# A hybrid attention block: products of coming units drawn in behind each transpose

## The chip, the cores and the metric

The kernel runs on one core of one Trainium2 chip. The metric is the device time of one execution in microseconds. The core has five engines with a queue each, which run side by side and wait for one another by semaphores: TensorE (PE; its weight loads are shown as PEld), VectorE (DVE), ScalarE (ACT), GpSimd (POOL) and SyncE (SP, which only issues DMA transfers here). An engine takes the instructions of its queue in the order in which the program has them.

## The reference, cut to what matters

One decoder layer on x of 512 rows by 1024 columns, in float32. A normalised copy h of x is multiplied by one wide matrix; its columns feed two attention branches (FoX, with forget terms, and MoBA, block-sparse), 8 heads of 64 columns each, a SiLU gate for each branch, and two merging gates.

```
h = rms_norm(x, norm_g)
fq, fk, fv, fz, mq, mk, mv, mz, ga, gb, fl = split_cols(h @ w_in, sizes)
y_fox  = from_heads(fox_attention(q, k, v, log_f)) * silu(fz)
...
y_moba = from_heads(moba_attention(q, k, v)) * silu(mz)
merged = sigmoid(ga + b_gate[0]) * (y_fox @ w_fox) + sigmoid(gb + b_gate[1]) * (y_moba @ w_moba)
out = x + merged @ w_out
```

## The kernel before

Matrices are kept as a high and a low part (tiles ending in h and l, or hi and lo), and a product in float32 is made of three matmuls: high by high, high by low, low by high.

The work comes in stages: the first loads and the normalisation; the first q, k, z and v columns (to about 60 us); attention; the gates with the second merge; the output projection.

**Attention.** Sixteen heads are done in four groups of four (FoX halves a and b, MoBA halves a and b), two pairs of heads in each. For a pair, `Tr` transposes its q and k columns (four 128x128 transposes into the PSUM tile `p_qT`, four into `p_kT`, L530 and L532) and ScalarE and VectorE make `QS`, `KH` and `KL` of them (L539 to L547; `Q` is cast at L557 for FoX). For a head, `Aa` makes four logits tiles `lg` of 128 rows by 128, 256, 384 and 512 columns (L572, L573), VectorE adds the mask and finds the row minimum (L575), ScalarE takes the exponential (L577). Then `Bb` transposes the ten non-zero 128x128 blocks of the probabilities (`blk`, L617): four into `p_a`, four into `p_b`, two into `p_cc`. ScalarE copies each of these tiles into a high part `pth` (L623), VectorE makes the low part `ptl` (L624), and eight matmuls with the values make `pv` (L627, L628), which is summed into `ypair` (L652, L653). So a head has 10 transposes and a pair 8: 16 x 10 + 8 x 8 = 224.

**PSUM.** The tiles lie in banks that are shared by tag: three banks for `tp` (`p_qT`, `p_kT`, `p_a`, `p_b`, `p_cc`, `p_ri`), two for `lg`, two for `pj` (the units below), one for `pv`. A tile can be written only when the engines have read the tile that was in its bank.

**Units.** Between the steps of attention stand units of other work: `unit` (128 rows of a 256-column projection, 24 matmuls, L315 to L317, tile `pj_...`), `unit_z` (half of a SiLU gate, 24 matmuls of 512 columns, L414 to L416, `pz_...`) and `unit_f` (128 columns of the first merge, 12 matmuls of 512 columns, L696 to L698, `pf...`). `filler` turns the units of a list of names into functions: each first calls `pump`, which issues weight loads on SP and the splitting of weights (ACT L141, DVE L143: `wh_...`, `wl_...`) up to three steps ahead, then makes all its matmuls and the evacuation of its tile. `inter` alternates a group's steps with its units. The plan is: group fa with fqb, fkb, fvb, mqa; fb with mka, mva, mza; ma with mqb, mkb, mvb; mb with mzb, wf0, wf1, wf2. After the last group `seq(["wf3"])` makes the last unit pair of the first merge.

**Order.** The program is written in the order of these calls, and a scheduler then orders each engine's instructions by its own estimate of time; `tc.issue_after(i)` keeps what is issued inside the block behind instruction `i` on its engine. So products of a unit and transposes already mix in the program before, but most transposes stand in runs of 2 to 10.

Of the kernel before, what the change touches and what calls it, by code (L numbers as in the profile page):

```python
# [13 lines left out]
P = 128  # L14
# [3 lines left out]
KT = D // P  # L18
# [11 lines left out]
def fox_moba_kernel(ctx: ExitStack, tc, xT, x, w_in, w_fl, w_fox, w_moba, w_out, cst, rope, out):  # L30
# [274 lines left out]
        for i, (a, b) in enumerate(pairs):  # L305
            T.matmul(o, a, b, start=(i == 0), stop=(i == n - 1))

    def unit_mm(p, name, t, hfs=(0, 1), first=True, last=True):
        n = 264 if name == "fka" else CW
        for hf in hfs:  # L310
            hi, lo = chunks[name][hf]
            for k in range(4):
                kk = 4 * hf + k
                st = slice(t * P, (t + 1) * P)
                T.matmul(p[:, :n], Gh[:, kk, st], hi[:, k, :n], start=(kk == 0), stop=False)  # L315
                T.matmul(p[:, :n], Gh[:, kk, st], lo[:, k, :n], start=False, stop=False)
                T.matmul(p[:, :n], Gl[:, kk, st], hi[:, k, :n], start=False, stop=(kk == KT - 1))  # L317

    def evac_qk(p, name, t):
        if name not in QN:  # L320
# [75 lines left out]
    def unit(name, t):  # L396
        def go():
            p = pj(f"pj_{name}{t}")
            unit_mm(p, name, t)
# [7 lines left out]
    def tr_mm(p, name, c):  # L407
        cc = slice(c * P, (c + 1) * P)
        for hf in range(2):
            hi, lo = chunks[name][hf]  # L410
            for k in range(4):
                kk = 4 * hf + k
                gh, gl = Z[kk] if name[0] == "f" else (Gh[:, kk, :], Gl[:, kk, :])
                T.matmul(p, hi[:, k, cc], gh, start=(kk == 0), stop=False)  # L414
                T.matmul(p, hi[:, k, cc], gl, start=False, stop=False)
                T.matmul(p, lo[:, k, cc], gh, start=False, stop=(kk == KT - 1))  # L416

    ZS = {}

# [2 lines left out]
    def unit_z(name, c):  # L422
        def go():
            p = (tp if name == "fzb" else pj)(f"pz_{name}{c}")
            tr_mm(p, name, c)
# [12 lines left out]

    LR = con.tile([64, S], F32R, name="LR")
# [77 lines left out]
    def attn_group(br, half, gq, gk):  # L517
# [8 lines left out]
        def Tr(pr):  # L526
            def go():
                pq, pk = tp("p_qT"), tp("p_kT")
                for t in range(NT):
                    T.transpose(pq[:, t * P:(t + 1) * P], qn[:, t, pr * P:(pr + 1) * P], ident)  # L530
                for t in range(NT):
                    T.transpose(pk[:, t * P:(t + 1) * P], kn[:, t, pr * P:(pr + 1) * P], ident)  # L532
                for o in range(2):
                    h = 2 * pr + o
                    me, ot = (slice(0, HD), slice(HD, P)) if o == 0 else (slice(HD, P), slice(0, HD))
                    qs = t2("qs", 4, "QS", dt=F32R)
                    kh = t2("qs", 4, "KH", dt=F32R)
                    kl = KLt[o][pr]
                    A.activation(qs[me, :], pq[me, :], AF.Copy, scale=gq[me, :])  # L539
                    V.scalar_tensor_tensor(qs[ot, :], pq[me, :], gq[me, :], qs[me, :].bitcast(F32),  # L540
                                           op0=OP.mult, op1=OP.subtract)
                    A.activation(kh[me, :], pk[me, :], AF.Copy, scale=gk[me, :])
                    if direct:
                        A.activation(kh[ot, :], pk[me, :], AF.Copy, scale=gk[me, :])  # L544
                    else:
                        nc.scalar.dma_start(out=kh[ot, :].bitcast(F32), in_=kh[me, :].bitcast(F32))
                    V.scalar_tensor_tensor(kl[me, :], pk[me, :], gk[me, :], kh[me, :].bitcast(F32),  # L547
                                           op0=OP.mult, op1=OP.subtract)
                    q2 = qs
                    if fox:  # L550
                        q2 = Q2t[o]
                        lr = slice(HD, HD + 4) if o == 0 else slice(0, 4)
                        hh = hb + h
                        nc.sync.dma_start(out=q2[lr, :].bitcast(F32), in_=LR[hh:32:8, :].bitcast(F32))
                        nc.sync.dma_start(out=kl[lr, :].bitcast(F32), in_=LR[32 + hh:64:8, :].bitcast(F32))
                        if direct:
                            V.tensor_copy(q2[me, :], qs[me, :].bitcast(F32))  # L557
# [52 lines left out]
        def Bb(h):  # L610
            def go():
# [2 lines left out]
                pv = pst("pv", 1, "pv")  # L614

                def blk(dst, i, j):
                    T.transpose(dst, pts[i][:, j * P:(j + 1) * P], ident)  # L617
# [70 lines left out]

    FS, MG = {}, {}

    def br_mm(p, name, br, c):
        hi, lo = chunks[name][0]
        cc = slice(c * P, (c + 1) * P)
        for k in range(4):
            yh, yl = Y[br, k]
            T.matmul(p, hi[:, k, cc], yh, start=(k == 0), stop=False)  # L696
            T.matmul(p, hi[:, k, cc], yl, start=False, stop=False)  # L697
            T.matmul(p, lo[:, k, cc], yh, start=False, stop=(k == 3))  # L698

    def unit_f(i, c):  # L700
        def go():
            j = 2 * i + c
            p = pj(f"pf{j}")
            br_mm(p, f"wf{i}", "f", c)
# [128 lines left out]
    def merge_a(i, c):  # L833
        if True:
            j = 2 * i + c
            p = pj(f"pm{j}")
            br_mm(p, f"wm{i}", "m", c)
# [183 lines left out]
            return [unit_z(name, c) for c in range(2)]  # L1021
        return [unit(name, t) for t in range(4)]

    def filler(names):
        res = []
        for nm in names:
            for n, u in enumerate(units(nm)):
                def go(i=first_prep[nm] + (n if nm[0] == "G" else 0), u=u):
                    pump(i)
                    u()  # L1030
                res.append(go)
        return res

    def inter(a, b):
# [30 lines left out]
    for k, u in enumerate(fz):  # L1065
        u()
        if k < 3:
# [169 lines left out]
```

## Time and profile before

| what | value |
|---|---|
| median of 3 runs | 425.61 us (425.08 to 425.87) |
| the profiled execution's own time | 425.94 us |
| its span, first to last instruction | 424.2 us |
| granted TensorE clock | 0.999 |
| instructions | 7682 |
| HBM read, written | 48.11 MB, 6.32 MB |

Lines of a timeline give the start and the duration of an instruction (or of a run of like ones, xN) in microseconds, its engine, its line in the kernel, the tile it writes and those that it reads, and its shape. The duration of a matmul reaches to where its result is written, so matmuls overlap one another: what one costs TensorE is read from start to start. A line of a group gives the count, the busy time in us, the mean of one in ns, and the idle time of its engine just before with what ended it.

### The profile page before, as it was taken

The page shows a single profiled execution, that of the slowest core. Times are in us where ns is not written, and L with a number is a line of the kernel's source. Part 1 is how long each engine was busy: PE and PEld are TensorE (multiplying, and loading weights), DVE is VectorE, ACT ScalarE, POOL GpSimd, SP SyncE. Part 2 cuts the span into 40 slices and gives each one's busy share as a digit, 9 for nine tenths or more (in the row PEclk, how much of TensorE's full clock was granted, in tenths as well). Part 3 has the DMA queues.
Part 4 walks back from the last instruction along what each step waited for, and adds up shares of the span by engine and source line. Part 5 has one row for each costly group of instructions (what it writes and reads, how often), then busy time and mean ns, then how long its engine had stood idle before and what let it go on. Part 6 is the DMA issues. An engine that isn't in the chain of part 4 may idle for free.

```text
span 424.2 us, 7682 instructions
## 1 busy us (share of the span) xinstructions
PE 417.8 (98%) x2913; PEld 388.6 (92%) x2913; DVE 327.4 (77%) x574; ACT 279.2 (66%) x527; POOL 103.8 (24%) x120
## 2 busy tenths in 40 slices
PE   8999999999999999999999999999999999999996
PEld 6998899999999998899998888899999989988885
DVE  3779977799967778678666679767979698689883
ACT  4976326778777878569757687656756535686450
POOL 1065630225235550015660100340000000022230
PEclk9999999999999999999999999999999999999999
DMA  7972334667253033212032310673052703697484
GB/s 233 392 281 87 112 100 111 181 206 199 74 176 114 26 102 100 80 45 99 27 100 68 106 53 27 229 250 117 24 178 62 236 2 110 208 259 118 99 140 159
DMA packets 24340, 56.10 MB, mean 132 GB/s; under 512 B 2808, under 2 KB 7600, under 8 KB 24304
## 3 DMA queue, kind: packets, MB, share of 16 engines
q1 hardware_dynamic: 13392, 38.11, 27.9%
q0 software_dynamic: 3392, 8.39, 8.7%
q10 hardware_dynamic: 7520, 9.11, 6.7%
q8 instruction: 23, 0.38, 0.4%
q14 instruction: 13, 0.11, 0.1%
HBM read 48.11 MB, written 6.32 MB: 128 GB/s over the span
## 4 chain that ended last, share of the span: by engine, by line
PE 96%; DMA 1%; SPq 0%; DVE 0%; issue 0%; ACT 0%
PE pb_GB L770 3%; PE pb_GA L770 3%; PE pb_GA L767 3%; PE pb_GB L767 3%; PE pb_GB L769 3%; PE pb_GA L769 3%; PE po L958 3%; PE po L957 3%; PE po L956 3%; PE pv L628 2%; PE lg L573 2%; PE pv L627 2%; PE lg L572 2%; PE pf L697 2%; PE pf L696 2%; PE pm L698 2%
## 5 line engine op out<-in xcount | busy, mean ns | idle before, releaser
L343 POOL TENSOR_TENSOR ff<-ss,mh 128x8 f32<-128x8 f32 x16 | 31.6, 1981 | 71.4 <-DVE ss L341 62.9
L575 DVE CUSTOM_DVE_ANT_0 p<-lg,mask 128x128 f32<-128x128 f32 (+1 forms) x64 | 30.9, 487 | 16.1 <-PE lg L573 15.6
L577 ACT ACTIVATE p<-p,negm 128x128 f32<-128x128 f32 (+1 forms) x64 | 35.7, 559 | 10.9 <-DVE negm L575 10.0
L905 POOL DMA_DIRECT2D wr_o<-in_w_out_dram x4 | 4.9, 1294 | 95.5 <-ACT wr_o L904 95.5
L143 DVE TENSOR_TENSOR wl_GA<-wr_ga,wh_GA 128x1024 fp32r<-128x1024 f32 x14 | 16.9, 1223 | 5.8 <-ACT wh_GA L141 3.9
L141 ACT ACTIVATE wh_GA<-wr_ga 128x1024 fp32r<-128x1024 f32 x14 | 14.7, 1061 | 9.9 <-PE pb_GA L769 5.1
L141 ACT ACTIVATE wh_GB<-wr_gb 128x1024 fp32r<-128x1024 f32 x14 | 14.6, 1059 | 9.5 <-PE pm L697 3.5
L918 ACT ACTIVATE wh_o<-wr_o 128x1024 fp32r<-128x1024 f32 x14 | 14.8, 1060 | 7.9 <-PE pb_GB L769 2.8
L572 PE MATMUL lg<-KH,QS 128*128 128x128 f32 (+1 forms) x64 | 20.0, 324 | 0.0
L919 DVE TENSOR_TENSOR wl_o<-wr_o,wh_o 128x1024 fp32r<-128x1024 f32 x14 | 17.0, 1222 | 3.8 <-ACT wh_o L918 3.8
L143 DVE TENSOR_TENSOR wl_GB<-wr_gb,wh_GB 128x1024 fp32r<-128x1024 f32 x14 | 16.9, 1222 | 3.5 <-ACT wh_GB L141 3.5
L653 DVE TENSOR_TENSOR ypair<-pv,ysh 64x512 f32<-64x512 f32 x16 | 11.0, 687 | 6.7 <-ACT ysh L652 6.3
L547 DVE SCALAR_TENSOR_TENSOR KL<-p_kT,cs,KH 64x512 fp32r<-64x512 f32 x16 | 12.0, 749 | 3.4 <-ACT KH L544 3.2
L652 ACT ACTIVATE ysh<-pv 64x512 f32<-64x512 f32 x16 | 9.5, 594 | 7.3 <-PE pv L628 4.2
L624 DVE TENSOR_TENSOR ptl<-p_a,pth 128x512 fp32r<-128x512 f32 x16 | 11.0, 685 | 4.2 <-ACT pth L623 4.2
L337 DVE TENSOR_REDUCE ss<-sq 128x8 f32<-128x512 f32 x16 | 10.9, 681 | 4.0 <-ACT sq L336 3.9
L767 PE MATMUL pb_GA<-Gh,wh_GA 128*128 128x256 f32 x48 | 13.6, 284 | 0.0
L769 PE MATMUL pb_GA<-Gl,wh_GA 128*128 128x256 f32 x48 | 13.5, 281 | 0.0
L770 PE MATMUL pb_GA<-Gh,wl_GA 128*128 128x256 f32 x48 | 13.5, 281 | 0.0
L770 PE MATMUL pb_GB<-Gh,wl_GB 128*128 128x256 f32 x48 | 13.5, 281 | 0.0
L769 PE MATMUL pb_GB<-Gl,wh_GB 128*128 128x256 f32 x48 | 13.4, 281 | 0.0
L767 PE MATMUL pb_GB<-Gh,wh_GB 128*128 128x256 f32 x48 | 13.3, 281 | 0.0
(461 smaller groups left out, 1801.8 us busy)
## 6 DMA issues: line engine op xcount, KB each, us to landing
wr_ga<-in_w_in_dram SPq DMA_DIRECT2D x8, 512.0 KB, 3.8
wr_gb<-in_w_in_dram SPq DMA_DIRECT2D x8, 512.0 KB, 4.6
wr_o<-in_w_out_dram SPq DMA_DIRECT2D x8, 512.0 KB, 11.4
xt<-in_xT_dram SPq DMA_DIRECT2D x8, 256.0 KB, 7.3
x<-in_x_dram SPq DMA_DIRECT2D x8, 256.0 KB, 6.0
s_dramh<-sum_sh ACTq DMA_DIRECT2D x8, 256.0 KB, 5.6
s_draml<-sum_sl ACTq DMA_DIRECT2D x8, 256.0 KB, 2.5
wr_wf<-in_w_fox_dram SPq DMA_DIRECT2D x4, 512.0 KB, 3.2
```

The source lines that it names most:

```text
L141: A.activation(hi[:, :, 0:n], src, AF.Copy)
L143: eng.tensor_tensor(out=lo[:, q, 0:n], in0=src[:, q], in1=hi[:, q, 0:n].bitcast(F32), op=OP.subtract)
L343: G.tensor_tensor(out=f2, in0=ss.rearrange("p t h -> p (t h)"), in1=mh, op=OP.pow)
L572: T.matmul(lg[:, :n], qs[:, qt], kh[:, :n], start=True, stop=False)
L575: V.tensor_tensor_reduce(pt, lg[:, :n], mask[:, 512 - n:512], -0.125, 3.0e38, op0=OP.add, op1=OP.min, accum_out=mkn[:, hh, i:i + 1])
L577: A.activation(pt, pt, AF.Exp, bias=mkn[:, hh, i:i + 1], scale=-1.0, accum_out=rs[:, hh, i:i + 1])
L767: T.matmul(o, hi[:, k, cc], lh, start=(n < 3 and c == 0 and k == 0), stop=False, skip_group_check=True)
L769: T.matmul(o, hi[:, k, cc], ll, start=False, stop=False, skip_group_check=True)
L770: T.matmul(o, lo[:, k, cc], lh, start=False, stop=(k == 3), skip_group_check=True)
L918: A.activation(wide(hi), wide(R[key, c]), AF.Copy)
L919: V.tensor_tensor(out=wide(lo), in0=wide(R[key, c]), in1=wide(hi).bitcast(F32), op=OP.subtract)
L956: T.matmul(o, gh, hi[:, c, r, :], start=(new and k == 0), stop=False, skip_group_check=True)
```

## The change

Every transpose of attention (`Tr` and `blk`) goes through `turn`. `turn` ties each transpose but the first of its group behind the instruction last issued on TensorE, and then takes one step in each of two turns in the first unfinished unit of `AHEAD`; the second step is tied behind the transpose. A step is one matmul of a unit, or, after its last matmul, the evacuation of its tile.

For this the three functions that made a unit's matmuls (`unit_mm`, `tr_mm`, `br_mm`) become generators of operand pairs, `products` issues one matmul at a time, and the units are objects (`Unit`) with `step` and `run`. `run` pumps as before and makes what is left of the unit. All units of the four groups are put in `AHEAD` in the plan's order; those of `wf3` are built, but are not put there, and are made after the last group.

```
+    def products(o, pairs):
+        pairs = list(pairs)
+        for i, (a, b) in enumerate(pairs):
+            if i:
+                yield
+            T.matmul(o, a, b, start=(i == 0), stop=(i == len(pairs) - 1))
...
+    AHEAD = []
+
+    def turn(o, i, first):
+        if first:
+            T.transpose(o, i, ident)
+        else:
+            with behind(mybir.EngineType.PE):
+                T.transpose(o, i, ident)
+        at = last_on(mybir.EngineType.PE)
+        for n in range(2):
+            while AHEAD and AHEAD[0].done:
+                AHEAD.pop(0)
+            if AHEAD:
+                if n:
+                    with tc.issue_after(at):
+                        AHEAD[0].step()
+                else:
+                    AHEAD[0].step()
+
+    class Unit:
+        def __init__(self, i, go):
+            self.i, self.go, self.it, self.done = i, go, None, False
+
+        def step(self):
+            if self.it is None:
+                self.it = self.go()
+            if self.it is None or next(self.it, self) is self:
+                self.done = True
+
+        def run(self):
+            pump(self.i)
+            while not self.done:
+                self.step()
...
-                    T.transpose(pq[:, t * P:(t + 1) * P], qn[:, t, pr * P:(pr + 1) * P], ident)
+                    turn(pq[:, t * P:(t + 1) * P], qn[:, t, pr * P:(pr + 1) * P], t == 0)
...
-                    T.transpose(pk[:, t * P:(t + 1) * P], kn[:, t, pr * P:(pr + 1) * P], ident)
+                    turn(pk[:, t * P:(t + 1) * P], kn[:, t, pr * P:(pr + 1) * P], False)
...
-                    T.transpose(dst, pts[i][:, j * P:(j + 1) * P], ident)
+                    turn(dst, pts[i][:, j * P:(j + 1) * P], j == 0 and i == 0)
...
+    fills = [filler(p[4], True) for p in plan]
+    wf3 = filler(["wf3"])
...
-        fill = filler(plan[n][4])
+        fill = fills[n]
...
-    seq(["wf3"])
+    for u in wf3:
+        u()
```

More of the change, by code (lines that the diff above doesn't have):

```diff
@@ L306, in mm3, with unit_mm @@
             T.matmul(o, a, b, start=(i == 0), stop=(i == n - 1))
-    def unit_mm(p, name, t, hfs=(0, 1), first=True, last=True):
+    def unit_mm(name, t):
         n = 264 if name == "fka" else CW
[L310 to L317, printed above, removed]
+        st = slice(t * P, (t + 1) * P)
+        for kk in range(KT):
+            hi, lo = (w[:, kk % 4, :n] for w in chunks[name][kk // 4])
+            gh, gl = Gh[:, kk, st], Gl[:, kk, st]
+            yield from ((gh, hi), (gh, lo), (gl, hi))
+    def products(o, pairs):
[4 more added lines that the diff above has]
+            T.matmul(o, a, b, start=(i == 0), stop=(i == len(pairs) - 1))
     def evac_qk(p, name, t):
@@ L398, in go @@
             p = pj(f"pj_{name}{t}")
-            unit_mm(p, name, t)
+            yield from products(p[:, :264 if name == "fka" else CW], unit_mm(name, t))
             if name[1] == "v":
@@ L404, in unit, with tr_mm @@
         return go
-    def tr_mm(p, name, c):
+    def tr_mm(name, c):
         cc = slice(c * P, (c + 1) * P)
[L409 to L416, printed above, removed]
+        for kk in range(KT):
+            hi, lo = (w[:, kk % 4, cc] for w in chunks[name][kk // 4])
+            gh, gl = Z[kk] if name[0] == "f" else (Gh[:, kk, :], Gl[:, kk, :])
+            yield from ((hi, gh), (hi, gl), (lo, gh))
     ZS = {}
@@ L424, in go @@
             p = (tp if name == "fzb" else pj)(f"pz_{name}{c}")
-            tr_mm(p, name, c)
+            yield from products(p, tr_mm(name, c))
             z = t2("y", 15, f"zs_{name}{c}")
@@ L695, in br_mm @@
             yh, yl = Y[br, k]
[L696 to L698 removed]
+            yield from ((hi[:, k, cc], yh), (hi[:, k, cc], yl), (lo[:, k, cc], yh))
     def unit_f(i, c):
@@ L703, in go @@
             p = pj(f"pf{j}")
-            br_mm(p, f"wf{i}", "f", c)
+            yield from products(p, br_mm(f"wf{i}", "f", c))
             if j == 0:
@@ L836, in merge_a @@
             p = pj(f"pm{j}")
-            br_mm(p, f"wm{i}", "m", c)
+            for _ in products(p, br_mm(f"wm{i}", "m", c)):
+                pass
             u = SG[i][:, c, :]
@@ L1027, in filler @@
             for n, u in enumerate(units(nm)):
[L1028 to L1031, printed above, removed]
+                x = Unit(first_prep[nm] + (n if nm[0] == "G" else 0), u)
+                if ahead:
+                    AHEAD.append(x)
+                res.append(x.run)
         return res
```

4 lines of the change are left out of this document (2 added, 2 removed).

## The prediction

> **What bounds the kernel now.** I read the page first, its busy shares and the chain of work that ended last.
>
> ```profile
> span 424.2 us, 7682 instructions
> ...
> PE 417.8 (98%) x2913; PEld 388.6 (92%) x2913; DVE 327.4 (77%) x574; ACT 279.2 (66%) x527; POOL 103.8 (24%) x120
> ...
> PE 96%; DMA 1%; SPq 0%; DVE 0%; issue 0%; ACT 0%
> ```
>
> TensorE carries 96% of the chain. The stage that the change touches begins near 60 us and ends near 276; the view by stretches splits the span there.
>
> ```profile
> 60.00:276.00 216.00, 216.00 (x1576) 203.50 (x1575) 165.08 (x350) 161.30 (x344) 62.71 (x72) 1.00 0.34 106
> 276.00:424.00 148.00, 144.58 (x986) 133.55 (x984) 115.57 (x132) 81.59 (x116) 16.16 (x17) 1.00 0.51 140
> ```
>
> The columns are stretch, its length, then PE, weight loads, DVE, ACT, POOL, granted clock, DMA. TensorE is never idle in the 216 us, at full clock, so the change can gain only if the same instructions take less TensorE time. A busy PE does not prove this, because matmul ends are modelled; so I read the timeline for distances between starts. First four transposes in a row, in a stream of 256-column products:
>
> ```profile
> 72.47 0.29 PE L317 MATMUL pj_fqb<-wh_fqb,Gl 128*128 128x256 f32 x1
> 72.59 0.60 PE L530 MATMUL p_qT<-ident,qn_fqa 128*128 128x128 f32 x4
> 72.95 0.36 PE L315 MATMUL pj_fqb<-wh_fqb,Gh 128*128 128x256 f32 x1
> 73.15 0.28 PE L316 MATMUL pj_fqb<-wl_fqb,Gh 128*128 128x256 f32 x1
> ```
>
> A 256-column product holds TensorE for 0.12 us (72.47 to 72.59). From the first transpose to 73.15 are 0.56 us; less 0.12 for the one product in it, the four took 0.44, 0.11 each. (The product behind a run is recorded early, so one must read on to the next start.) Now a transpose that already stands alone between products:
>
> ```profile
> 204.50 0.27 PE L617 MATMUL p_a<-ident,p 128*128 128x128 f32 x1
> 204.53 0.37 PE L317 MATMUL pj_mkb<-wh_mkb,Gl 128*128 128x256 f32 x1
> 204.73 0.28 PE L315 MATMUL pj_mkb<-wh_mkb,Gh 128*128 128x256 f32 x1
> ```
>
> 204.50 to 204.73 are 0.23; less 0.12 it cost 0.11 too. So the price of a transpose does not depend on what stands beside it.
>
> **The change part by part.** Sixteen heads with 10 transposes and eight pairs of heads with 8 make 224 transposes that now pull up to two products of the coming units behind them. No product, transpose or byte is added or removed; TensorE has 2911 matmuls in the program before and after. Runs of two to ten transposes become some 200 single ones. At 0.11 each way this is worth 0.00 us. The second product is tied behind its transpose, and each transpose but the first of its group behind the one before it. These ties are an order within TensorE's own queue, not semaphores, so they cost nothing themselves. The generators in place of the loops change nothing on the chip. Keeping wf3 apart only says that no transpose may draw its products early; they still come after the last heads. Up to 60 us the order is unchanged, and from the gates on it is the same again but for the four transposes of p_rinv. About a hundred instructions each on ScalarE and VectorE change places by a few positions, DMA issues of the inverse sums and of the sums' stores among them; on SP one 4-row load of the forget terms moves ahead of the two mqb weight loads; POOL's few moved steps (a power, a rope addition, a multiplication by the inverse sums, two memsets) have 153 of 216 us free. I cost these at nothing under the cover of a full TensorE; if one came late, the pair of heads that reads it would start late.
>
> What is not free: products that filled waits are used up inside the runs of transposes, and what follows a run comes nearer to it. TensorE then reaches instructions whose operands ScalarE and VectorE have not finished, and everything behind waits, the drawn products included. I went through the changed order and looked for places where less TensorE work than chain stands between cause and use. Three stand out.
>
> Place 1, third MoBA head (before: 219 us).
>
> ```profile
> 218.90 0.47 PEld L617 LDWEIGHTS p_a<-ident,p 128*128 128x128 f32 x4
> 219.00 0.60 PE L617 MATMUL p_a<-ident,p 128*128 128x128 f32 x4
> 219.63 0.60 ACT L623 ACTIVATE pth<-p_a 128x512 fp32r<-128x512 f32 x1
> 220.27 0.69 DVE L624 TENSOR_TENSOR ptl<-p_a,pth 128x512 fp32r<-128x512 f32 x1 [0.23 <-ACT pth L623]
> 222.50 0.39 PE L627 MATMUL pv<-pth,v_mva 128*128 128x512 f32 x1
> ```
>
> The transposes' slots end at 219.00 + 4 x 0.11 = 219.44, and the p_a bank is free at 220.96, 1.52 later. The next pair's p_qT and p_kT hold the other two banks of the three, so p_b takes this bank. Before, some 4 us of work stood between. After, there are three 256-column products (0.35) and one 512-column product.
>
> ```profile
> 201.74 0.40 PE L628 MATMUL pv<-ptl,v_mva 128*128 128x512 f32 x1
> 201.97 0.27 PE L597 MATMUL p_ri<-ident,rinv 128*8 128x128 f32 x1
> ```
>
> That is 0.23, together 0.58. TensorE waits 1.52 - 0.58 = 0.94, and 0.1 more because a transpose's weights load 0.10 ahead of it (218.90 to 219.00): 1.04. Behind it stand the drawn mvb products, which nothing else holds. Bounds: 0.8 if ScalarE and VectorE start without a gap, 1.6 if another 0.6 us operation is in their way.
>
> Place 2, second pair of the FoX half b. From its last p_qT transpose to the fifth logits product, which needs the bank of the third, the new order has 44 products of 256 columns (5.3), 15 transposes (1.6), four of 512 (0.9) and five short ones (0.8): 8.6 us; before it was about 17. In that time VectorE must run, in its order, QS, cast, wl_mza, KL, QS, cast, the 128 mask step, wl_mza, the 256 step, ptl, KL, the sums of squares and the 384 step:
>
> ```profile
> L540 DVE SCALAR_TENSOR_TENSOR QS<-p_qT,cs,QS 64x512 fp32r<-64x512 f32 x16 | 12.0, 750 | 1.5 <-ACT QS L539 1.0
> L547 DVE SCALAR_TENSOR_TENSOR KL<-p_kT,cs,KH 64x512 fp32r<-64x512 f32 x16 | 12.0, 749 | 3.4 <-ACT KH L544 3.2
> L624 DVE TENSOR_TENSOR ptl<-p_a,pth 128x512 fp32r<-128x512 f32 x16 | 11.0, 685 | 4.2 <-ACT pth L623 4.2
> L337 DVE TENSOR_REDUCE ss<-sq 128x8 f32<-128x512 f32 x16 | 10.9, 681 | 4.0 <-ACT sq L336 3.9
> L575 DVE CUSTOM_DVE_ANT_0 p<-lg,mask 128x384 f32<-128x384 f32 x16 | 8.9, 555 | 4.2 <-PE lg L573 3.9
> L575 DVE CUSTOM_DVE_ANT_0 p<-lg,mask 128x256 f32<-128x256 f32 x16 | 6.7, 420 | 4.0 <-PE lg L573 4.0
> L575 DVE DVE_READ_ACCUMULATOR2_ANT negm<- 128x1 f32 x64 | 5.3, 83 | 0.0
> L575 DVE CUSTOM_DVE_ANT_0 p<-lg,mask 128x128 f32<-128x128 f32 x16 | 4.6, 288 | 3.5 <-PE lg L573 3.3
> L143 DVE TENSOR_TENSOR wl_mza<-wr_mza,wh_mza 128x1024 fp32r<-128x1024 f32 x2 | 2.5, 1226 | 0.8 <-ACT wh_mza L141 0.7
> L557 DVE CAST Q<-QS 64x512 fp32r<-64x512 f32 x4 | 2.1, 536 | 0.1
> L539 ACT ACTIVATE QS<-p_qT,cs 64x512 fp32r<-64x512 f32 x16 | 10.9, 682 | 2.8 <-DVE QS L540 1.6 <-PE lg L572 0.9
> ```
>
> The sum is 2 x 0.750 + 2 x 0.536 + 2 x 1.226 + 2 x 0.749 + 0.685 + 0.681 + 0.288 + 0.420 + 0.555 + 3 x 0.083 = 9.4. Neighbours overlap by 0.08 (below, 138.12 + 0.55 against 138.59); fifteen such seams leave 8.2.
>
> ```profile
> 138.12 0.55 DVE L575 CUSTOM_DVE_ANT_0 p<-lg,mask 128x384 f32<-128x384 f32 x1
> 138.59 0.08 DVE L575 DVE_READ_ACCUMULATOR2_ANT negm<- 128x1 f32 x1
> ```
>
> Before it starts, the transposes land (0.2) and ScalarE copies QS (0.68): 9.1 against 8.6, so 0.5 us of waiting. Bounds 0 and 1.2 (one more 1.2 us split in the way).
>
> Place 3, second MoBA pair of half b: from its last p_kT transpose to the first transpose into p_b stand 3.8 us of TensorE work (13 products of 512 columns at 0.23, the rest short); VectorE has two weight steps, KL and QS before the bank is free.
>
> ```profile
> L143 DVE TENSOR_TENSOR wl_GA<-wr_ga,wh_GA 128x1024 fp32r<-128x1024 f32 x14 | 16.9, 1223 | 5.8 <-ACT wh_GA L141 3.9 <-PE pv L628 2.0
> L731 DVE TENSOR_TENSOR wr_ga<-wr_ga,wr_ga 128x1024 f32<-128x1024 f32 x8 | 9.8, 1221 | 0.1
> ```
>
> 1.22 + 1.22 + 0.75 + 0.75 - 0.24 = 3.7. It decides whether they start at once; I take 0.35, between 0 and 1.2.
>
> The sum is 1.04 + 0.5 + 0.35 = 1.9. The profiled run took 425.94 (span 424.2 and 1.7 around it); the median is 0.33 lower, so 425.61 + 1.9 = 427.5. Bounds of the three together: +0.8 and +4.0.
>
> **The rivals.** (a) Hidden transposes, faster. Transposes might run at 0.11 only because each one's weights must load, and two products could cover that load. The price if covered is that of a 128-column product whose successor is ready:
>
> ```profile
> 210.35 0.22 PE L572 MATMUL lg<-KH,QS 128*128 128x128 f32 x1
> 210.41 0.28 PE L573 MATMUL lg<-KL,QS 128*128 128x128 f32 x1
> ```
>
> 0.06, so 200 x 0.05 = 10 us less: 415.6. It decides from the first single transpose on. Against it stands the one at 204.50, and that four in a row cost four times 0.11, the last one, with a product behind it, included. [...]
>
> (b) No change, 425.6. The view of before shows room: at place 1 the bank was free 1.5 us ahead of the pv product. If ScalarE and VectorE reach the chains earlier than I add them up, only part of place 1 is left, under 0.85 us. For: places 2 and 3 are close calls. Against: place 1 needs no queue to be late.
>
> (c) More places, slower still. VectorE is nearly full where the first heads run:
>
> ```profile
> 80.00:100.00 20.00, 20.00 (x164) 19.62 (x164) 18.53 (x43) 17.55 (x43) 3.06 (x4) 1.00 0.54 155
> 100.00:120.00 20.00, 20.00 (x165) 19.69 (x165) 19.12 (x39) 15.94 (x32) 7.58 (x5) 1.00 0.51 155
> ```
>
> 18.5 and 19.1 of 20. If TensorE gets ahead there, two to four more waits of about 0.8 follow: 429.9. Against: before, banks there came free over 2 us early.
>
> **How the numbers follow.** Forecast 52%, (a) 8%, (b) 24%, (c) 16%. About 0.2% (0.85 us) can be told from no change. Slower: 0.52 + 0.16 = 0.68. Faster: (a) and a sixth of (b), 0.12. Same: 0.20. The range 425.0 to 429.5 holds the forecast, nearly all of (b) and half of (c). The forecast's own range is 426.5 to 429.
>
> **What would show it.** Single transposes at 0.11 start to start confirm the zero; 0.06 is rival (a). The first p_b transpose of the third MoBA head with about 1 us of TensorE idle ahead, released by ptl, confirms place 1. Idle near the fifth logits product of the FoX pair and ahead of p_b in half b confirms 2 and 3. Unchanged length from 276 us to the end shows that nothing moved there. The prediction fails if TensorE stays gapless in 60 to 276, or if that stretch shortens.

## The result and the profile after

| | before | after |
|---|---|---|
| median of the runs taken together | 425.58 us (425.08 to 425.87) | 432.78 us (432.2 to 433.25), 4 runs |
| the profiled execution | 425.94 us, span 424.2 | 432.71 us, span 430.8 |

The ratio is 1.017, with an interval of 1.0152 to 1.0187. The change makes the kernel slower, as forecast, but by 7.2 us and not by 1.9; 432.78 lies outside the range. One of the eleven executions of the last variant below took 1458.27 us, for a reason that is not known; its median counts it, its ratio does not. The page of after, its shares of busy time and of the chain that ended last:

```profile
PE 421.9 (98%) x2913; PEld 388.3 (90%) x2913; DVE 330.4 (77%) x574; ACT 277.9 (65%) x527; POOL 104.6 (24%) x120
...
PE 91%; DMA 3%; DVE 2%; ACT 2%; issue 1%; SPq 0%; ACTq 0%
```

The busy shares hardly move (PE 98% both times). The chain does: TensorE's part falls from 96% to 91%, and those of transfers (1% to 3%), VectorE and ScalarE (0% to 2% each) rise. The view by stretches, for the same stage and for the stage behind it (6 us later than in before):

```profile
60.00:276.00 216.00, 213.53 (x1544) 197.81 (x1544) 162.08 (x339) 155.79 (x334) 61.90 (x69) 1.00 0.31 96
282.00:430.00 148.00, 145.17 (x989) 134.07 (x987) 116.20 (x133) 82.19 (x116) 16.16 (x17) 1.00 0.51 142
```

In 216 us TensorE does 1544 matmuls where it did 1576, still at full clock. The last 148 us hold 989 where they held 986, and from the start of the last `pv` product (281.52 in before, 288.12 in after) to the end are 142.7 us both times: nothing moved there. The idle time recorded is only 2.5 us, because a matmul's recorded end lies beyond its slot (0.28 us recorded for a 256-column product, and the next start 0.12 behind its own). The list of what weight loads waited for shows more (engine, line, what it waited for: us in total, times, longest). In before it has rows of the start alone; in after these stand behind such rows:

```profile
PEld lg L609 <- DVE negm L612: 1.1, 2, 0.6
PEld pv L664 <- ACT pth L660: 0.9, 2, 0.5
...
PEld lg L609 <- issue: 0.8, 1, 0.8
PEld lg L610 <- DVE KL L584: 0.6, 1, 0.6
PEld p_b L448 <- DVE ptl L661: 0.5, 1, 0.5
...
PEld pj_mvb L322 <- DVE v_mvb L358: 0.3, 1, 0.3
```

Each is read exactly from start to start, less the slot of the first instruction (0.06 for 128 columns, 0.12 for 256, 0.18 for 384, 0.23 for 512, 0.11 for a transpose):

| time in after | what waits | measured | predicted |
|---|---|---|---|
| 75.8 to 77.0 | first logits of attention, for the copy of KH | 1.05 | none |
| 146.8 to 153.6 | place 2, four waits | 2.35 | 0.5 |
| 199.6 to 200 | logits in MoBA half a | 0.26 | none |
| 223.4 to 224.7 | place 1 | 0.98 | 1.04 |
| 230.1 to 230.9 | third MoBA head's end, for the value columns | 0.45 | none |
| 259.5 to 260.7 | place 3 | 0.71 | 0.35 |

Together 5.8 of the 6.6 us that the span grew. Another 0.25 lies ahead of attention (the first sums of the forget terms start at 60.29 us and not at 60.04), and about half a microsecond is spread over attention in steps too small to see one by one. Most of it can be found as an average: the 202 single transposes of attention in after that have a product of 256 or 512 columns behind them take 0.1125 us each, those in 42 runs of before 0.1101, and 0.0024 times some 200 is 0.5 us. No run tests this share by itself. The timeline of TensorE in after at place 2 (start, duration, engine, line, tiles; the bracket holds the idle time before and what ended it):

```profile
142.40 0.27 PE L448 MATMUL p_qT<-ident,qn_fqb 128*128 128x128 f32 x1
...
146.59 0.39 PE L609 MATMUL lg<-KH,QS 128*128 128x128 f32 x2
147.41 0.50 PE L610 MATMUL lg<-KL,Q 128*128 128x128 f32 x2 [0.43 <-DVE KL L584]
147.75 0.28 PE L322 MATMUL pj_mva<-wh_mva,Gh 128*128 128x256 f32 x1
148.29 0.30 PE L448 MATMUL p_b<-ident,p 128*128 128x128 f32 x1 [0.27 <-DVE QS L577]
...
148.55 0.27 PE L448 MATMUL p_b<-ident,p 128*128 128x128 f32 x1
148.58 0.36 PE L322 MATMUL pj_mva<-wl_mva,Gh 128*128 128x256 f32 x1
148.78 0.28 PE L322 MATMUL pj_mva<-wh_mva,Gl 128*128 128x256 f32 x1
148.90 0.28 PE L448 MATMUL p_b<-ident,p 128*128 128x128 f32 x1
...
150.07 0.40 PE L664 MATMUL pv<-pth,v_fvb 128*128 128x512 f32 x1
150.68 0.50 PE L609 MATMUL lg<-KH,QS 128*128 128x512 f32 x1 [0.21 <-DVE negm L612]
...
152.72 0.42 PE L664 MATMUL pv<-pth,v_fvb 128*128 128x384 f32 x1
153.38 0.33 PE L609 MATMUL lg<-KH,QS 128*128 128x128 f32 x1 [0.25 <-DVE negm L612]
```

First the price: from the transpose at 148.55 to the next at 148.90 are 0.35 us with two products of 0.12 between them, so a transpose that stands alone costs 0.11, as in a run. Then the waits: after a 256-column product at 147.75 the next start should be 147.87 and is 148.29; after the 512-column product at 150.07 it should be 150.30 and is 150.68. VectorE is what they wait for each time; its timeline in the same place:

```profile
143.43 0.74 DVE L577 SCALAR_TENSOR_TENSOR QS<-p_qT,cs,QS 64x512 fp32r<-64x512 f32 x1 [1.69 <-ACT QS L576]
144.20 0.52 DVE L594 CAST Q<-QS 64x512 fp32r<-64x512 f32 x1
144.75 1.95 DVE L143 TENSOR_TENSOR wl_mza<-wr_mza,wh_mza 128x1024 fp32r<-128x1024 f32 x1
146.63 0.73 DVE L584 SCALAR_TENSOR_TENSOR KL<-p_kT,cs,KH 64x512 fp32r<-64x512 f32 x1
147.39 0.76 DVE L577 SCALAR_TENSOR_TENSOR QS<-p_qT,cs,QS 64x512 fp32r<-64x512 f32 x1
148.18 0.63 DVE L594 CAST Q<-QS 64x512 fp32r<-64x512 f32 x1
...
152.76 0.56 DVE L612 CUSTOM_DVE_ANT_0 p<-lg,mask 128x384 f32<-128x384 f32 x1
153.25 0.08 DVE L612 DVE_READ_ACCUMULATOR2_ANT negm<- 128x1 f32 x1
```

VectorE has no idle time from 143.43 to 153.33: here it is the bound. The weight split at 144.75 took 1.95 us.

Place 1 in after, TensorE and, in the second fence, VectorE:

```profile
223.30 0.28 PE L322 MATMUL pj_mvb<-wh_mvb,Gl 128*128 128x256 f32 x1
223.90 0.50 PE L664 MATMUL pv<-pth,v_mva 128*128 128x512 f32 x1 [0.32 <-ACT pth L660]
224.63 0.33 PE L448 MATMUL p_b<-ident,p 128*128 128x128 f32 x1 [0.23 <-DVE ptl L661]
```

```profile
223.88 0.69 DVE L661 TENSOR_TENSOR ptl<-p_a,pth 128x512 fp32r<-128x512 f32 x1 [0.70 <-ACT pth L660]
```

The transpose into p_b starts when `ptl` has ended (223.88 + 0.69 = 224.57). The wait is 0.60 - 0.12 = 0.48 ahead of pv and 0.73 - 0.23 = 0.50 behind it.

Place 3 in after, the weight loads that waited and, in the second fence, VectorE:

```profile
259.87 0.19 PEld L664 LDWEIGHTS pv<-pth,v_mvb 128*128 128x128 f32 x1 [0.34 <-ACT pth L660]
260.36 0.19 PEld L322 LDWEIGHTS pf<-yhf,wh_wf 128*128 128x128 f32 x1 [0.30 <-ACT f L745]
```

```profile
259.93 0.76 DVE L577 SCALAR_TENSOR_TENSOR QS<-p_qT,cs,QS 64x512 fp32r<-64x512 f32 x1
```

Both wait for ScalarE, which works from 257.12 to 260.30 without a pause: pv for its `pth`, which ends at 259.82, and pf for its bank, which ScalarE's copy `f` has read at 260.30. The transpose into p_b, which was to wait for VectorE, does not: VectorE's chain ends with QS at 260.69, the transpose's weights load at 260.83 with no wait and it starts at 260.92. Without the 0.71 us ahead of it the transpose would have come at 260.21 and waited 0.48 for QS; that is an estimate from these times.

The wait that was not foreseen, at 76 us in after. In FoX half a, and there alone, half of `KH` is not made by ScalarE but by a DMA copy of the other half, issued on ScalarE's queue. TensorE, and ScalarE's queue with the issue:

```profile
75.68 0.28 PE L322 MATMUL pj_fqb<-wh_fqb,Gl 128*128 128x256 f32 x1
76.59 0.30 PE L609 MATMUL lg<-KH,QS 128*128 128x128 f32 x1 [0.64 <-DMA KH<-KH]
```

```profile
69.04 0.69 ACT L579 ACTIVATE KH<-p_kT,cs 64x512 fp32r<-64x512 f32 x1 [0.65 <-PE p_kT L448]
70.21 0.39 ACT L327 ACTIVATE qn_fqb<-pj_fqb 128x256 f32<-128x256 f32 x1 [0.49 <-PE pj_fqb L322]
70.27 0.47 ACTq L583 DMA_DIRECT2D KH<-KH  x1
```

The same issue in before, and the logits that read it:

```profile
68.79 0.86 ACTq L546 DMA_DIRECT2D KH<-KH  x1
```

```profile
74.92 0.22 PE L572 MATMUL lg<-KH,QS 128*128 128x128 f32 x1
```

The copy is issued 1.48 us later than in before. About 1.0 of it is that `KH` itself starts at 69.04 and not at 68.03, since the transposes for it, with two products behind each, end later. The other 0.5 is ScalarE's queue: in before the issue came 0.1 us behind the end of `KH`, here 0.54, behind the evacuation of a unit (`qn_fqb`) for which ScalarE waited 0.49. The logits were due at 75.68 + 0.12 = 75.80, only 0.88 later than in before. The copy, some 6 us from issue to use, is late.

### The profile page after: what moved, and what is told of

Read it like the earlier page. It is cut to its first block, busy times and chain, and to the rows that moved or that the text cites. A ratio compares the mean times of both kernels' runs of the same rounds, so it can differ in the third digit from the quotient of the medians.

```text
span 430.8 us, 7677 instructions
## 1 busy us (share of the span) xinstructions
PE 421.9 (98%) x2913; PEld 388.3 (90%) x2913; DVE 330.4 (77%) x574; ACT 277.9 (65%) x527; POOL 104.6 (24%) x120
## 4 chain that ended last, share of the span: by engine, by line
PE 91%; DMA 3%; DVE 2%; ACT 2%; issue 1%; SPq 0%; ACTq 0%
PE pm L322 5%; PE pf L322 5%; PE pb_GB L805 3%; PE pb_GA L805 3%; PE pb_GB L802 3%; PE pb_GB L804 3%; PE pb_GA L802 3%; PE pb_GA L804 3%; PE po L994 3%; PE po L993 3%; PE po L992 3%; PE pj_fkb L322 3%; PE pj_fva L322 3%; PE pj_mkb L322 3%; PE pj_mqa L322 3%; PE pj_mqb L322 3%
## 5 line engine op out<-in xcount | busy, mean ns | idle before, releaser
L609 PE MATMUL lg<-KH,QS 128*128 128x128 f32 (+1 forms) x64 | 20.0, 332 | 1.1 <-DMA KH<-KH 0.6
L448 PE MATMUL p_b<-ident,p 128*128 128x128 f32 x64 | 16.4, 273 | 0.5 <-DVE QS L577 0.3
L577 DVE SCALAR_TENSOR_TENSOR QS<-p_qT,cs,QS 64x512 fp32r<-64x512 f32 x16 | 12.0, 750 | 6.1 <-ACT QS L576 5.8
L609 PEld LDWEIGHTS lg<-KH,QS 128*128 128x128 f32 x64 | 11.8, 188 | 2.8 <-DVE negm L612 1.1
L661 DVE TENSOR_TENSOR ptl<-p_b,pth 128x512 fp32r<-128x512 f32 x16 | 11.0, 686 | 4.3 <-ACT pth L660 4.1
L342 DVE TENSOR_REDUCE ss<-sq 128x8 f32<-128x512 f32 x16 | 10.9, 679 | 4.2 <-ACT sq L341 4.1
L322 PE MATMUL pf<-yhf,wh_wf 128*128 128x512 f32 x32 | 13.8, 431 | 0.0
```

The lines of the kernel that those rows point to most:

```text
L322: T.matmul(o, a, b, start=(i == 0), stop=(i == len(pairs) - 1))
L448: T.transpose(o, i, ident)
L609: T.matmul(lg[:, :n], qs[:, qt], kh[:, :n], start=True, stop=False)
```

## The experiments

Twelve variants were run against the kernel before, whose median was 425.21 us beside eight of them and 425.33 beside the other four (second product untied, no draws in FoX half b, no draws in MoBA half a, first group's units). The start of the program varies by up to 1.2 us from one profiled execution to another (below), so the last column leaves it out: it is the time from the first sum of the forget terms to the last `pv` product in the profiled execution, less the 221.48 us of before (60.04 to 281.52). After has 6.35 there (60.29 to 288.12).

| variant | median us | ratio to before, interval | attention, us over before |
|---|---|---|---|
| ties, nothing drawn | 425.36 | 0.9996 (0.998 to 1.0012) | 0.00 |
| one product behind each transpose | 426.03 | 1.0018 (1.0009 to 1.0028) | 0.59 |
| draws without ties | 428.71 | 1.0081 (1.0066 to 1.0096) | 3.81 |
| draws without ties, not the last group's units | 425.94 | 1.0019 (1.001 to 1.0028) | 0.47 |
| second product untied | 430.21 | 1.0113 (1.0096 to 1.013) | 5.20 |
| heads' transposes only | 428.98 | 1.0088 (1.0073 to 1.0103) | 3.25 |
| pairs' transposes only | 432.2 | 1.0157 (1.0134 to 1.0181) | 5.33 |
| no copy by DMA | 431.0 | 1.0127 (1.011 to 1.0143) | 5.25 |
| no GpSimd multiplication for mka | 430.96 | 1.0139 (1.0119 to 1.0159) | 5.75 |
| no draws in FoX half b | 429.41 | 1.0091 (1.0077 to 1.0104) | 4.29 |
| no draws in MoBA half a | 431.11 | 1.0132 (1.0118 to 1.0146) | 5.31 |
| first group's units only, no copy by DMA | 425.95 | 1.0009 (1.0 to 1.0019) | 0.84 |

**Is it the ties, or the single transposes?** The ties stay, nothing is drawn:

```
-    fills = [filler(p[4], True) for p in plan]
+    fills = [filler(p[4]) for p in plan]
```

> All transposes go through turn and keep their ties behind one another, but no unit is put in AHEAD, so nothing is drawn; on TensorE 26 instructions stand elsewhere than in the kernel before, nowhere else one. Theory (a tie costs nothing, the loss comes from the products that are drawn into the runs and then lack as cover further on): 425.2 to 425.7, the time of the kernel before, and no weight load of attention that waits. Rival (the ties themselves cost TensorE): 224 tied transposes by some 0.03 us are 6 us, about 432.

425.36 us, no difference from before, and the list of waiting weight loads has the three start-up rows only. Attention takes as long as in before. The ties cost nothing by themselves.

One product behind each transpose instead of two:

```
-        for n in range(2):
+        for n in range(1):
             while AHEAD and AHEAD[0].done:
```

> One product behind each transpose instead of two; 109 transposes stand alone. If waits come from the missing cover at a few places, half the draws leave room at most of them: 426 to 428 us. If each single transpose had a price of its own (about 0.03 us each), the loss goes with the number of single ones: 425.6 + 7.2 x 98/202 = 429.1 us.

426.03 us, at the lower edge of what was expected and just clear of before. In its program 109 transposes stand alone (213 in after), and the only wait of attention in its list of weight loads is one of 0.2 us. Had the loss gone with the number of single transposes, it would have been 429.1. So standing alone costs a transpose some thousandths of a microsecond at most and does not make it cheaper; what costs are the waits.

**Where do the draws cost?** Draws stay, all ties are taken away, so that the scheduler places the products where its own estimate wants them:

```
-        if first:
-            T.transpose(o, i, ident)
-        else:
-            with behind(mybir.EngineType.PE):
-                T.transpose(o, i, ident)
-        at = last_on(mybir.EngineType.PE)
+        T.transpose(o, i, ident)
...
-                if n:
-                    with tc.issue_after(at):
-                        AHEAD[0].step()
-                else:
-                    AHEAD[0].step()
+                AHEAD[0].step()
```

> Products are drawn at the same transposes, but neither the transposes nor the second product is tied, so the scheduler is free to place them; 74 transposes stand alone instead of 213. Theory (the loss is waiting where a tied run brings TensorE to its operands too early): with freedom to put other work ahead, most waits go, 425.3 to 427.5 us. Rival (the drawn products themselves, by using up the later cover, make the loss, tied or not): 430 us or more.

428.71 us, between the theory and the rival. The timeline of TensorE in this variant has one place for it:

```profile
279.58 0.38 PE L444 MATMUL p_cc<-ident,p 128*128 128x128 f32 x2
282.28 0.79 PE L655 MATMUL pv<-pth,v_mvb 128*128 128x512 f32 x1 [2.32 <-DVE ypair L681]
```

The last head waits for VectorE to empty the one bank of `pv`, and no unit is left to fill the wait: 2.70 less two transposes, 2.5 us. In before, 24 products into `pb_GA` (277.42 to 280.36) stand between the last p_cc and that pv, and in after 17; here all 24 are done by 277.4, ahead of the last head, since the `pf` products that stood there before had been spent earlier, at transposes that did not need them. The wait is not the whole price. In this execution TensorE's granted clock is at half behind it, as the view by stretches shows in the last column but two:

```profile
282.20:285.20 3.00, 2.92 (x10) 2.73 (x11) 0.36 (x2) 0.17 (x1) 1.80 (x3) 0.50 1.01 359
```

The products from 282.28 to 285.4 take some 1.5 us longer than at their slots. The same kernel without the last group's units in `AHEAD`:

```
-    fills = [filler(p[4], True) for p in plan]
+    fills = [filler(p[4], i < 3) for i, p in enumerate(plan)]
```

> The kernel of the untied draws, with the units of the last group (mzb, wf0 to wf2) not put in AHEAD. Theory (its loss of 3.5 us is the one wait of 2.5 us for ypair at 280 us, at the end of attention, where the drawn units are used up): that wait is gone and the time is 425.3 to 426.2. Rival (draws in the first three groups cost as well, the wait at the end only moves): 427.5 or more.

425.94 us, within 0.2% of before: the wait is gone, and the draws of the first three groups cost at most half a microsecond where the scheduler may place them.

Only the second product untied, in after; the ties of the transposes stay:

```
-        at = last_on(mybir.EngineType.PE)
...
-                if n:
-                    with tc.issue_after(at):
-                        AHEAD[0].step()
-                else:
-                    AHEAD[0].step()
+                AHEAD[0].step()
```

> After, with the second product no longer tied behind its transpose (the transposes stay tied behind one another), so that the scheduler may put the drawn products where it expects a wait; 109 transposes stand alone instead of 186. Theory (what costs is that products are spent at the transposes): fewer are spent there, so less than after, 427 to 430, and a part of it as a wait for the last heads after 275 us, as in the kernel of the untied draws. Rival (the number of drawn products sets the loss, not where they are tied): 432 or more.

430.21 us, between after and the kernel without any tie. Its list of waits has the KH wait (1.1) and 3.2 us for `ypair` in two waits, 0.9 at 184 us and 2.3 at 282 us: places 1, 2 and 3 are gone, and the end of attention pays most. By the count used above 109 transposes stand alone in it, and 213 in after, not 186.

Drawing at the heads' transposes only:

```
-                    turn(pq[:, t * P:(t + 1) * P], qn[:, t, pr * P:(pr + 1) * P], t == 0)
+                    T.transpose(pq[:, t * P:(t + 1) * P], qn[:, t, pr * P:(pr + 1) * P], ident)
...
-                    turn(pk[:, t * P:(t + 1) * P], kn[:, t, pr * P:(pr + 1) * P], False)
+                    T.transpose(pk[:, t * P:(t + 1) * P], kn[:, t, pr * P:(pr + 1) * P], ident)
```

> Only the 160 transposes of the heads' probabilities draw products; those of q and k stand in runs as before. Theory: the waits near the logits of a new pair (76 us, 147 us, 260 us in the changed kernel) come from drawing at q and k, since the products there stood before between the transposes and the first logits; about 4 us of the 7.2 go, 428 to 429.5 us. Rival (loss grows with the number of drawn products alone, 160 of 224): 430.5 us.

428.98 us, as expected in the time. Its waits lie at 140 to 160, 220 to 240 and 260 to 280 us, and there is none at 76.

Drawing at the pairs' transposes only:

```
-                    turn(dst, pts[i][:, j * P:(j + 1) * P], j == 0 and i == 0)
+                    T.transpose(dst, pts[i][:, j * P:(j + 1) * P], ident)
```

> Only the 64 transposes of q and k draw products. Theory: it keeps the waits at the logits of a new pair, 428.5 to 430 us. Rival (loss by number, 64 of 224): 427.6 us.

432.2 us, more than expected. The four executions differ, from 430.34 to 432.71, and the profiled one is the fastest, inside the band but for 0.3 us. Its list of waits:

```profile
PEld pv L664 <- DVE ypair L690: 2.8, 2, 2.5
...
PEld lg L609 <- issue: 1.2, 1, 1.2
PEld pv L665 <- DVE ptl L661: 0.9, 1, 0.9
```

It keeps the KH wait, has one of 0.9 us for `ptl` at 107 us, and has the one for `ypair` at 282 us, which after has not. The three slower executions have a mean granted clock of 0.992 to 0.995 and the profiled one 0.998, so part of the median may be a halved clock behind that wait, as above; they have no trace. The two halves lose 3.8 and 7.0 us, and 3.25 and 5.33 by the last column, together more than the whole with its 7.2 and 6.35: the losses do not add up.

**The wait for KH.** The keys of the first half are written as those of the others, by ScalarE and VectorE, with no DMA copy on ScalarE's queue:

```
-        direct = br + half != "fa"
+        direct = True
```

> After, with the keys of the first FoX half written by ScalarE and VectorE as those of the other halves are, not by the DMA copy on ScalarE's queue (L583). Theory (the wait of about 1.0 us of the logits for KH at 75.7 to 77 us is that copy, late behind the stores of the sums on the same queue): that wait is gone, 431.3 to 432.0 against the 432.7 of after. Rival (ScalarE and VectorE are as late with the keys, and the wait only changes its name): 432.5 or more.

431.0 us, and the row `lg L609 <- issue` is gone from its waits, while all others of after stay. The profiled runs differ by 1.51 us (432.71 against 431.2): 1.05 is this wait, and 0.39 lies ahead of attention, where this run's forget sums start at 59.90 us (on this start, see the next experiment).

**Place 2: is the split slow because of GpSimd?** The multiplication of mka by the inverse sums is left out (so the keys of MoBA half a are not normalised); TensorE, VectorE and ScalarE keep the order of after:

```
-        G.tensor_tensor(out=q3, in0=q3, in1=f2[:, :, None].to_broadcast([P, 8, HD]), op=OP.mult)
+        if name != "mka":
+            G.tensor_tensor(out=q3, in0=q3, in1=f2[:, :, None].to_broadcast([P, 8, HD]), op=OP.mult)
```

> After, without GpSimd's multiplications by the inverse sums for mka (L350); the order on TensorE, VectorE and ScalarE is that of after. It leaves out the normalisation of the keys of MoBA's half a. Theory (the split wl_mza took 1.95 us instead of 1.23 at 144.75 because GpSimd worked on the same moment, and place 2 is as large as it is by that): the split takes 1.23 to 1.4, the waits from 146.7 to 153.7 shrink from 2.4 to 1.5 to 1.8 us, the time is 431.8 to 432.3. Rival (the split is slow for another reason): 432.7, and the split still at 1.9.

VectorE's row for the split in this variant:

```profile
143.57 1.37 DVE L143 TENSOR_TENSOR wl_mza<-wr_mza,wh_mza 128x1024 fp32r<-128x1024 f32 x1
```

1.37 instead of 1.95, and place 2, summed as above, shrinks from 2.35 to 1.7 us. So some 0.6 us of it came from the multiplication that ran beside the split. The time fell by more, 1.87 us between the profiled runs (432.71 against 430.84); the other 1.2 lie ahead of attention, and by the last column the variant gains 0.60. In all these kernels the order up to 60 us is the same, but the time that the start takes is not: the first sums of the forget terms, in after and in this variant,

```profile
60.29 0.30 PE L521 MATMUL p_c<-fg,triU 128*128 128x32 f32 x2
```

```profile
59.12 0.30 PE L522 MATMUL p_c<-fg,triU 128*128 128x32 f32 x2
```

stand 1.17 us apart. The time of a single variant therefore tells the worth of a place to about one us only, and the rows of the place and the last column of the table decide. Why the start varies stays open.

**Do the other places stand and fall with the draws?** Drawing is suspended during one turn of the loop over the groups, first for FoX half b (`n != 1`), then for MoBA half a (`n != 2`); the ties stay:

```
-    AHEAD = []
+    AHEAD, DRAW = [], [True]
...
-        for n in range(2):
+        for n in range(2 if DRAW[0] else 0):
...
+        DRAW[0] = n != 1
```

> After, with drawing suspended while the group of FoX half b is done (the second turn of the loop over the groups); the ties stay. Theory (the four waits of place 2, 2.35 us together between 146.7 and 153.7 us, come from the 256-column products that are drawn there and are missing later in the same pair): the four are gone and nothing takes their place, 430.2 to 430.9, with 16.0 - 2.4 = 13.6 us of TensorE time above the slot prices, or less. Rival (the missing cover shows up at a later place): 432 or more.

429.41 us, below the expected band. The profiled runs differ by 3.39 us: 2.35 of place 2 and 1.16 of an earlier start (the forget sums at 59.13), less 0.3 by which the wait for KH, ahead of this group, is longer here (1.1 against 0.8 in the list). The stretch in this variant:

```profile
140.00:160.00 20.00, 20.00 (x167) 19.69 (x166) 15.64 (x35) 15.68 (x36) 13.67 (x19) 1.00 0.20 67
```

TensorE is without a gap where after had 18.85 of 20 us. Place 2 is gone whole, and nothing behind it took its place: places 1 and 3 have their old sizes.

> After, with drawing suspended while the group of MoBA half a is done (the third turn of the loop). Theory (place 1, 0.98 us at 223 to 224.6 us, and the small waits of 0.45 us at 230 us come from the products drawn in this group): both are gone, 430.9 to 431.6, and place 2 stays at 2.2 to 2.5 us. Rival (place 1 comes from the bank alone, whatever is drawn): 432.3 or more, with ptl still releasing the transpose into p_b.

431.11 us, in the band, but partly by an earlier start (forget sums at 59.70, 0.59). Both waits are gone, yet the trace gained less than their sum, because place 3 grew from 0.71 to 1.73 us:

```profile
256.68 0.39 PE L609 MATMUL lg<-KH,QS 128*128 128x128 f32 x2
257.76 0.49 PE L610 MATMUL lg<-KL,QS 128*128 128x128 f32 x2 [0.69 <-DVE KL L584]
```

In after, pv and a product stand between the two pairs of logits; here the KL logits come straight behind the KH ones and 0.90 us wait for VectorE (257.76 - 256.68 - 0.18). What one wait less upstream won came back in part downstream. Whether by the missing wait or by the other order of TensorE's instructions at this place, no run separates.

Last, the draws of the first group alone, without the DMA copy:

```
-    fills = [filler(p[4], True) for p in plan]
+    fills = [filler(p[4], i < 1) for i, p in enumerate(plan)]
...
-        direct = br + half != "fa"
+        direct = True
```

> After, with the units of the first group alone in AHEAD and the keys of FoX half a written by ScalarE and VectorE instead of the DMA copy. Theory (single transposes between two drawn products cost what they cost in a run, and without a wait the interleaving is neutral): 425.2 to 426.2. Rivals: single transposes are cheaper, under 424.8; the draws of the first group cost something besides the wait for KH, 426.8 or more.

425.95 us: neutral within what can be told. 73 transposes stand alone in it, and its one new wait above 0.3 us is 0.4 for a value tile, which is half of the 0.84 in the last column. No variant beats the kernel before.

## Why the prediction was right in direction and wrong in size

**The price of a transpose: right.** 0.11 predicted, 0.11 measured from start to start. "Worth 0.00" held to about half a microsecond, since on average the price is 0.1125 alone and 0.1101 in a run. Rival (a), 0.06 a piece and 10 us less, is refuted by after, by the one-product variant and by the first-group variant alike.

**Ties, generators, the stage from the gates on: right.** The variant with ties alone equals before; the last 148 us hold as many matmuls as before.

**Place 1: right.** 1.04 predicted, 0.98 measured, released by `ptl` as said. From the last p_a transpose's slot to the end of `ptl` are 1.52 us, as in the working. Half of the wait already stands one instruction earlier, at pv, which needs `pth` of the same tile.

**Place 2: the term that failed most, 0.5 against 2.35**, and beyond its bound of 1.2. The TensorE side of the comparison was right: from the last p_qT transpose (142.40) to the fifth logits product (153.38) are 10.98 us, and without the waits up to there 8.7, where I had 8.6. The chain was mis-sized: 9.1 predicted, 10.9 measured. Of the 1.8, 0.8 are longer operations (the split 1.95 for 1.23, the casts 1.15 for 1.07), since the means of before hold no such meeting with GpSimd as this place has: the two splits of mza took 1.23 us each in before, and no GpSimd operation ran beside them (none from 144.4 to 152.5). Another 0.9 are the seams: I took fifteen overlaps of 0.08 from one pair of rows, a mask step and its read-out. Most seams here are the other way: QS ends at 144.17 and the cast starts at 144.20. The durations in after add up to 10.2 and took 9.9; the seams save 0.3, not 1.2. The last 0.15 is the start, 1.03 from the transpose to VectorE's QS against 0.88. And the wait does not come at one instruction: TensorE meets VectorE at KL, at QS and twice at `negm`.

**Place 3: the place was right, the cause in after is another, and the size is luck.** 0.71 lies inside the bounds of 0 to 1.2, but it was to be idle time ahead of p_b, until VectorE's QS had freed the bank, and there is none there. ScalarE holds TensorE first, at pv and at pf. Its steps had been left out of the sum. The VectorE chain itself was summed well: without ScalarE's waits it would have cost an estimated 0.48. In the variant without draws in MoBA half a, where the order differs, VectorE's KL is what TensorE waits for.

The three places together measure 4.04, just over the 4.0 that was given as their upper bound; that alone would have brought 429.6. The rest of the 7.2 lies outside the sum.

**The term put at nothing that was not nothing: the moved ScalarE steps and DMA issues.** The prediction said that displaced ScalarE steps and DMA issues lie "under the cover of a full TensorE". At 76 us they don't: a group of transposes with two products behind each takes 0.35 us a piece and not 0.11, so its readers start later; the copy's issue then stands behind a unit's evacuation on ScalarE's queue, and a copy of some 6 us from issue to use has no room for the 1.48 us. That is 1.05 us, and without the copy it is gone. I had named the consequence (the pair that reads it starts late) without working out the one chain that contains a DMA. The waits of 0.26 and 0.45 in MoBA half a were not looked for either.

**Rivals (b) and (c).** (b), no change, is refuted. (c) came nearer to the time, 429.9, for a reason that fell: it put further waits at 80 to 120 us, where VectorE is nearly full, and after has none there. They lie where a single chain is long, not where the engine's average is high. The pairs-only variant does have one such wait, 0.9 us at 107, so (c) was not groundless.

So the mechanism, used-up cover, is shown by the suspended draws: without them in a group, that group's waits are gone. The steps that failed are two: the chain of place 2, undersized by 1.8, and the moved work put at nothing. Three places were missing (1.76 together): 1.05 is the moved copy, and the other 0.71 go with the draws of MoBA half a, without which they are gone; which step of their chains is late was not worked out. The last half microsecond of the 6.6 has the size of 200 single transposes at 0.0024 us more each; that no other small thing is in it is not shown.

## What to carry to other kernels

Interleaving did not make a transpose cheaper here, 0.11 us alone as in a run; it only moved work that was filling waits. Before a tie fixes where filler goes, find for each group the shortest distance between a producer's chain and its use, and add up the chain from the rows of that place, with its own seams and neighbours, not from means of the whole kernel. Add up ScalarE's chain as well as VectorE's, and look for any DMA in them. Filler is a stock: spent early it was missing here at the last head, where nothing was left to replace it (a wait of 2.5 us with the draws untied), and a wait removed upstream may come back downstream (place 3, 1.73 us and not 0.71 without the draws of MoBA half a).

## What the runs showed of the hardware that was not expected

At place 2 VectorE and GpSimd both took longer side by side. In after, GpSimd's multiplication runs from 144.40 to 145.62, and an addition behind it takes 1.44 us, where the same step for mka takes 0.46:

```profile
144.40 1.22 POOL L350 TENSOR_TENSOR qn_mka<-qn_mka,ff 128x512 f32<-128x512 f32 x1
145.58 1.44 POOL L386 TENSOR_TENSOR qn_mqa<-ra,rb 128x128 f32<-128x128 f32 x1
```

```profile
148.07 0.46 POOL L386 TENSOR_TENSOR qn_mka<-ra,rb 128x128 f32<-128x128 f32 x1
```

VectorE's split starts at 144.75 and ends at 146.70, which is 1.08 behind the end of the multiplication; the addition ends at 147.02, 0.32 behind the end of the split. The split's 1.95 are near its own 1.23 plus the 0.87 that the multiplication still ran, and without the multiplication it took 1.37; there another GpSimd operation still ran 0.28 us into it (143.21 to 143.85), and the addition behind that took 1.44 again and ended 0.31 behind the split. That each waits for the other to finish would fit these rows; no run shows it. Without the multiplication place 2 cost TensorE some 0.6 us less (1.7 for 2.35), since the split stood in the chain that TensorE waited for.

A wait of 2.5 us cost more than its length here, though not in every execution. In the variant with draws without ties, TensorE stood idle for 2.5 us up to 282.28, and the profile has its granted clock at 0.50 from 282.20 to 285.20; the first products of 512 columns there lie 0.43 to 0.59 us apart and not 0.23. The two executions of that kernel with a mean clock of 0.996 took 429.08 and 429.25 us, the two with 1.0 took 428.35 and 427.86. In the profiled execution of the pairs-only variant, with a wait as long (2.5 us in the list), the mean clock is 0.998. What decides between the two is not shown here.
